# A SwiGLU's gate and up projections by two-by-two blocks with seven products, on the second half of the tokens

## The chip, the cores and the metric

The kernel runs on one core of a Trainium2 chip. The metric is the device time of one execution in microseconds (us), smaller is better. The engines are called by their names: TensorE (PE in the rows) multiplies matrices, VectorE (DVE) and GpSimd (POOL) work elementwise, ScalarE (ACT) computes functions and copies, SyncE (SP) issues transfers (DMAs) between HBM and SBUF. PSUM is the memory that TensorE writes its sums to, in 8 banks.

## What is computed

One step of a hybrid decoder layer for 1024 prompt tokens and 8 sample tokens with a model width of 1024: attention and a recurrent part, an output projection, then a normed, modulated input `h2` to a SwiGLU feed-forward part with 2816 columns:

```python
h2  = modulate(rms_norm(x), ...)
ffn = (silu(h2 @ w_ffn_gate) * (h2 @ w_ffn_up)) @ w_ffn_down   # 1024 -> 2816 -> 1024
x   = x + gate2 * ffn
```

Everything is fp32. The change touches the feed-forward part alone, and of it the second half of the tokens.

## The kernel before, in words

The feed-forward part is computed for two halves of the tokens, one after the other: half A with 512 tokens, half B with 512 prompt tokens and the 8 sample tokens, 520 columns, taken as 256 and 264. The 2816 columns are 22 blocks of 128, worked on in pairs, so 11 pairs for B.

An fp32 product is emulated with three products of a faster format. Every operand is split into a high part (a rounded copy) and a low part (what the rounding left), and high x high, high x low and low x high are added up in PSUM (`mm_fm`, L264 to L272, matmul L270). So each weight tile needs three steps in `wtile`: a load of 512 KB (L1644), ScalarE's high copy (L1648) and the subtraction for the low part (L1649), which `self.loe` does, GpSimd in half B. The same is done to tokens (`h2hi`, `h2lo`) and activations (`ah`, `al`).

For each of a pair's two blocks `ffn` multiplies gate and up weights by the tokens (8 blocks of 128 rows x 3 products x 2 parts of the columns), applies Silu on ScalarE (L1673), multiplies on VectorE out of PSUM (L1674) and splits the result (L1675, L1676). Then come the down products of the pair (L1685, 96 matmuls) and VectorE's additions to eight accumulators (L1696). The last pair of B scales its sums by `gate2` and writes the rows out (`ffn_rows`: transposes L1740, additions L1741, stores L1742).

A's last steps, scaling (L1718) and `ffn_rows`, stand in the code between B's first pair and the others. B's tokens come from `out_part` (L1530 to L1635), which ends with the splitting of the sample tokens at L1635. The code gives each engine's work in an order that a scheduler then rearranges; at run time each engine follows its own order, and semaphores hold it back where a buffer or an input isn't ready. Tiles live in pools; a name has as many buffers as `bufs` says, and a new tile of that name waits until the oldest is no longer read. A pool that is opened after others were closed takes their memory and waits for what used it.

## Time and profile before

| what | us |
|---|---|
| median of 3 runs (lowest to highest) | 2057.04 (2055.04 to 2057.09) |
| the profiled execution | 2053.88 |
| its span in the profile | 2051.8 |
| TensorE busy | 1924.1 (94%) |
| VectorE, ScalarE, GpSimd busy | 1213.6, 808.2, 728.8 |
| gate, up and other products of `mm_fm` on the chain (L270) | 37% |
| down products on the chain (L1685) | 11% |

The profile shows one execution. The span runs from the first to the last recorded instruction; some us of the execution lie outside it. The mean granted clock of TensorE was 0.965 of full speed. Half B's pairs fill the program from about 1650 us to the end, so the stretches of the trace that matter here lie behind 1560 us.

### The profile page before, as it was taken

What the parts mean: (1) busy time and instruction counts of PE and PEld (TensorE: products, weight loads), DVE (VectorE), ACT (ScalarE), POOL (GpSimd) and SP (SyncE); (2) the same over time, 40 slices, a digit from 0 to 9 for tenths busy, and PEclk for the clock granted to TensorE, in tenths of its full rate; (3) what the DMA queues carried; (4) which work ended last, traced back from release to release, by engine and by line L of the source; (5) the groups of instructions that cost most, each with busy time, mean ns of one, the idle gap of its engine ahead of it and who ended that gap; (6) DMA issues with size and microseconds to landing.
All of it is one profiled execution on the core that took longest, in us unless ns stands there. A gap on an engine that the chain in (4) does not pass through costs nothing.

```text
span 2051.8 us, 39068 instructions
## 1 busy us (share of the span) xinstructions
PE 1924.1 (94%) x15050; PEld 1649.1 (80%) x15050; DVE 1213.6 (59%) x3024; ACT 808.2 (39%) x1646; POOL 728.8 (36%) x1347
## 2 busy tenths in 40 slices
PE   4999999999999989899969999999999999999998
PEld 3878898999976667677659777777768989999998
DVE  7777988886646656676645554677644452222225
ACT  5466676643324445455433422322213322222221
POOL 2411244100033456466444303012214444545452
PEclk9999999999998979899979999999999999999999
...
GB/s 265 88 32 31 54 104 104 114 146 91 71 126 188 186 106 49 82 71 45 51 151 93 95 82 131 120 115 141 134 102 222 133 49 154 93 90 93 88 93 112
DMA packets 303720, 220.30 MB, mean 107 GB/s; under 512 B 67663, under 2 KB 282162, under 8 KB 303534
## 3 DMA queue, kind: packets, MB, share of 16 engines
...
q8 instruction: 118, 1.93, 0.4%
...
q10 hardware_dynamic: 18, 0.04, 0.0%
...
## 4 chain that ended last, share of the span: by engine, by line
PE 76%; DVE 10%; DMA 5%; ACT 3%; issue 3%; POOL 1%; SPq 1%; DVEq 0%; ACTq 0%; POOLq 0%
PE ps L270 37%; PE ps L1685 11%; PE ps L1574 5%; PE ps L1272 3%; PE ps L1261 2%; DVE sc L563 2%; PE ps L1062 2%; PE ps L1241 1%; PE ps L973 1%; PE ps L388 1%; PE ps L183 1%; DMA d_x<-ox 1%; DMA d_t<-arr 1%; PE ps L1242 1%; DVE fl L1649 1%
## 5 line engine op out<-in xcount | busy, mean ns | idle before, releaser
L1648 ACT ACTIVATE fh<-fr 128x1024 fp32r<-128x1024 f32 (+1 forms) x183 | 191.6, 1056 | 519.8 <-PE ps L270 289.0
L270 PE MATMUL ps<-h2hi,fh 128*128 128x264 f32 (+2 forms) x1056 | 341.9, 326 | 9.7 <-ACT fh L1648 6.4
L270 PE MATMUL ps<-h2hi,fl 128*128 128x264 f32 (+2 forms) x1056 | 338.0, 325 | 8.7 <-DVE fl L1649 8.7
L270 PE MATMUL ps<-h2lo,fh 128*128 128x512 f32 (+2 forms) x1056 | 340.0, 323 | 0.5 <-POOL h2lo L1623 0.5
L1649 POOL TENSOR_TENSOR fl<-fr,fh 128x1024 fp32r<-128x1024 f32 (+1 forms) x95 | 229.9, 2426 | 283.7 <-ACT fh L1648 277.6
L270 PE MATMUL ps<-h1hi,fh 128*128 128x344 f32 (+1 forms) x752 | 247.9, 330 | 4.0 <-ACT y L932 2.7
L270 PE MATMUL ps<-h1hi,fl 128*128 128x344 f32 (+1 forms) x752 | 244.3, 325 | 0.0
L270 PE MATMUL ps<-h1lo,fh 128*128 128x344 f32 (+1 forms) x752 | 244.3, 325 | 0.0
L270 PEld LDWEIGHTS ps<-h2hi,fh 128*128 128x128 f32 x1056 | 201.8, 191 | 30.9 <-ACT fh L1648 12.8
L270 PEld LDWEIGHTS ps<-h2hi,fl 128*128 128x128 f32 x1056 | 200.5, 191 | 29.5 <-DVE fl L1649 12.1
L270 PEld LDWEIGHTS ps<-h2lo,fh 128*128 128x128 f32 x1056 | 201.7, 191 | 14.5 <-POOL h2lo L1623 0.7
L1025 POOL TENSOR_TENSOR itmp<-la,arr 128x24 f32<-128x24 f32 (+23 forms) x496 | 129.4, 261 | 226.9 <-DMA la<-d_l 191.1
L1674 DVE TENSOR_TENSOR fa<-fa,ps 128x256 f32<-128x256 f32 (+1 forms) x66 | 33.8, 512 | 245.9 <-PE ps L270 245.2
L1685 PE MATMUL ps<-al,fh 128*128 128x512 f32 (+2 forms) x528 | 166.3, 321 | 1.1 <-DVE al L1676 1.0
L1685 PE MATMUL ps<-ah,fl 128*128 128x512 f32 (+2 forms) x528 | 160.7, 320 | 0.0
L1685 PE MATMUL ps<-ah,fh 128*128 128x512 f32 (+2 forms) x528 | 157.1, 322 | 1.2 <-ACT ah L1675 1.2
L1696 DVE TENSOR_TENSOR acc<-acc,ps 128x512 f32<-128x512 f32 (+2 forms) x224 | 107.8, 516 | 82.1 <-PE ps L1685 81.7
L270 PEld LDWEIGHTS ps<-h1hi,fh 128*128 128x128 f32 x752 | 141.4, 188 | 11.0 <-issue 3.6
L1649 DVE TENSOR_TENSOR fl<-fr,fh 128x1024 fp32r<-128x1024 f32 x88 | 108.5, 1233 | 70.1 <-ACT fh L1648 63.9
L1027 POOL TENSOR_TENSOR arr<-arr,itmp 128x24 f32<-128x24 f32 (+23 forms) x496 | 136.0, 274 | 38.3
L270 PEld LDWEIGHTS ps<-h1lo,fh 128*128 128x128 f32 x752 | 141.4, 188 | 4.3 <-issue 4.1
L270 PEld LDWEIGHTS ps<-h1hi,fl 128*128 128x128 f32 x752 | 141.4, 188 | 1.3 <-issue 1.2
...
## 6 DMA issues: line engine op xcount, KB each, us to landing
...
```

Of the source, the lines that this page charges most:

```text
L270: mm = nc.tensor.matmul(ps[:m, :n], a[:, k, wc:wc + m], b[:, k, t0:t0 + n], start=(k == 0 and i == 0), stop=(k == kd - 1 and i == 2))
L563: nc.vector.scalar_tensor_tensor(sc, r[:, :L], wcol, sc, op0=OP.mult, op1=OP.add)
L1025: ie.tensor_tensor(t3, bc(la[:, s, s + 1:][:, None, :], [128, nu, nt]), bc(arr[:, 0:nu, s:s + 1], [128, nu, nt]), op=OP.mult)
L1027: ie.tensor_tensor(arr[:, 0:nu, s + 1:], arr[:, 0:nu, s + 1:], t3, op=OP.subtract)
L1062: nc.tensor.matmul(pd[c % 2][E2[b], 128 * (c // 2):128 * (c // 2) + 128], w[i, c, :], x[i, c, :], start=True, stop=True)
L1261: nc.tensor.transpose(ps[:, 128 * (l % 4):128 * (l % 4) + 128], P[e][:, 128 * l:128 * l + 128], ident)
L1272: nc.tensor.matmul(po[o, 0:128], vt[:, l, o], PT[e][:, 128 * (l % 4):128 * (l % 4) + 128], start=(l == 0), stop=(l == i))
L1574: nc.tensor.matmul(p3[:, t, :], a[:, k, ts], b[:, k % 4, :], start=(k == 0 and n == 0), stop=(k == KD - 1 and n == 2))
L1648: nc.scalar.activation(hi, raw, AF.Copy)
L1649: self.loe.tensor_tensor(lo, raw, hi.bitcast(F32), op=OP.subtract)
L1685: self.lastmm = nc.tensor.matmul(ps[:, :n], a[:, 0, 128 * o:128 * o + 128], b[:, c:c + n], start=(i == 0), stop=(i == 5))
L1696: self.lastv = nc.vector.tensor_tensor(a, a, ps[:, :n], op=OP.add)
```

## The change

In half B the products of gate and up are taken in blocks of two by two: the 1024 rows are cut in two (4 blocks of 128 rows each), the pair's 256 columns in two, and the 520 tokens in two (256 and 264). Strassen's scheme, in the form with 15 additions, needs 7 products of such blocks where the direct way needs 8, and sums of blocks before and after.

- `quad_tokens` makes the sums of the token blocks once (16 additions on VectorE, with high copies on ScalarE and low parts on GpSimd), ahead of the pairs.
- `quad_weights` loads a pair's gate or up weights as one tile of 1 MB, makes four sums of blocks (`fs0` to `fs3`, one buffer each) on VectorE, and yields seven blocks of 128x512 with high and low parts (`fh`, `fl`, 8 buffers each).
- `quad_mm` runs the seven products, 12 matmuls each, and puts the four results together with seven additions on VectorE and one copy on ScalarE; `quad_gate_up` applies Silu, multiplies and splits, now from SBUF and 520 columns at a time.
- The down weights get names of their own (`dr`, `dh`, `dl`, two buffers each). The down products stay.
- B's weight pool `wfB` is opened only after the token sums, A's last rows and the closing of A's pools; all of B's pairs, the first too, stand behind A's rows.

```diff
--- before.py
+++ after.py
@@ -1635,21 +1635,119 @@
             nc.vector.tensor_tensor(lo[:, :, ts], f, hi[:, :, ts].bitcast(F32), op=OP.subtract)
-    def wtile(self, src, r0, c0, nr, ncol, wp):
+    def wtile(self, src, r0, c0, nr, ncol, wp, nm="f", nb=None):
...
-        nb = self.wbufs
-        raw = wp.tile([128, nr, ncol], F32, name="fr", bufs=nb[0])
+        nb = nb or self.wbufs
+        raw = wp.tile([128, nr, ncol], F32, name=nm + "r", bufs=nb[0])
...
-        hi = wp.tile([128, nr, ncol], F32R, name="fh", bufs=nb[1])
-        lo = wp.tile([128, nr, ncol], F32R, name="fl", bufs=nb[2])
+        hi = wp.tile([128, nr, ncol], F32R, name=nm + "h", bufs=nb[1])
+        lo = wp.tile([128, nr, ncol], F32R, name=nm + "l", bufs=nb[2])
         nc.scalar.activation(hi, raw, AF.Copy)
         self.loe.tensor_tensor(lo, raw, hi.bitcast(F32), op=OP.subtract)
         return hi, lo
-    def ffn(self, h, cols, fs, acc, wp, tp, pst, t0=None):
+    N2 = QT + NS
+    def quad_tokens(self, h, pool, tp):
+        nc, n = self.nc, self.N2
+        new = [[pool.tile([128, 4, n], F32R, name=f"q{i}{z}") for z in "hl"] for i in (2, 3, 4)]
+        t1 = [a[:, 0:4, QT:] for a in h]
+        for k in (0, 2):
+            ks = slice(k, k + 2)
+            b = []
+            for i in range(2):
+                for j in range(2):
+                    t = tp.tile([128, 2, n], F32, name=f"qb{i}{j}")
+                    w, kk, c = (n if j else QT), slice(4 * i + k, 4 * i + k + 2), (slice(QT, None) if j else slice(0, QT))
+                    if not j:
+                        nc.vector.memset(t[:, :, QT:], 0.0)
+                    nc.vector.tensor_tensor(t[:, :, 0:w], h[0][:, kk, c].bitcast(F32), h[1][:, kk, c].bitcast(F32), op=OP.add)
+                    b.append(t)
+            t = [tp.tile([128, 2, n], F32, name=f"qt{i}") for i in range(4)]
+            nc.vector.tensor_tensor(t[2], b[3], b[1], op=OP.subtract)
+            nc.vector.tensor_tensor(t[0], b[1], b[0], op=OP.subtract)
+            nc.vector.tensor_tensor(t[1], b[3], t[0], op=OP.subtract)
+            nc.vector.tensor_tensor(t[3], t[1], b[2], op=OP.subtract)
+            for x, (hi, lo) in zip(t, [t1] + new):
+                nc.scalar.activation(hi[:, ks, :], x, AF.Copy)
+                nc.gpsimd.tensor_tensor(lo[:, ks, :], x, hi[:, ks, :].bitcast(F32), op=OP.subtract)
+        return [t1] + new
+    def quad_weights(self, src, f0, wp):
+        nc = self.nc
+        cols = src.shape[-1]
+        raw = wp.tile([128, KD, 2, 128], F32, name="fr", bufs=2)
+        nc.sync.dma_start(raw.rearrange("p k f c -> p k (f c)"),
+                          bass.AP(tensor=src.tensor, offset=src.offset + 128 * f0, ap=[[cols, 128], [128 * cols, KD], [1, 256]]))
+        blk = lambda f, i: raw[:, 4 * i:4 * i + 4, f, :]
+        S = [wp.tile([128, 4, 128], F32, name=f"fs{i}", bufs=1) for i in range(4)]
+        nc.vector.tensor_tensor(S[0], blk(1, 0), blk(1, 1), op=OP.add)
+        nc.vector.tensor_tensor(S[1], S[0], blk(0, 0), op=OP.subtract)
+        nc.vector.tensor_tensor(S[2], blk(0, 0), blk(1, 0), op=OP.subtract)
+        nc.vector.tensor_tensor(S[3], blk(0, 1), S[1], op=OP.subtract)
+        for x in (blk(0, 0), S[1], blk(0, 1), S[2], S[0], S[3], blk(1, 1)):
+            hi = wp.tile([128, 4, 128], F32R, name="fh", bufs=8)
+            lo = wp.tile([128, 4, 128], F32R, name="fl", bufs=8)
+            nc.scalar.activation(hi, x, AF.Copy)
+            self.loe.tensor_tensor(lo, x, hi.bitcast(F32), op=OP.subtract)
+            yield hi, lo
+    def quad_mm(self, src, f0, out, h, T, wp, tp, pst):
+        nc, n = self.nc, self.N2
+        b = lambda i, j: [a[:, 4 * i:4 * i + 4, QT * j:QT * j + (n if j else QT)] for a in h]
+        w = self.quad_weights(src, f0, wp)
+        def prod(x, m):
+            (wh, wl), ps = next(w), pst.tile([128, 512], F32, name="ps")
+            for k in range(4):
+                for i, (u, v) in enumerate(((wh, x[0]), (wh, x[1]), (wl, x[0]))):
+                    nc.tensor.matmul(ps[:, :m], u[:, k, :], v[:, k, 0:m], start=(k == 0 and i == 0), stop=(k == 3 and i == 2))
+            return ps[:, :m]
+        v = nc.vector.tensor_tensor
+        new = lambda nm: tp.tile([128, n], F32, name=nm, bufs=2)
+        self.qn = self.qn + 1
+        m1 = self.qm[self.qn % 2]
+        nc.scalar.activation(m1[:, 0:QT], prod(b(0, 0), QT), AF.Copy)
+        u2, u3, u4 = new("u2"), new("u3"), new("u4")
+        v(u2, m1, prod(T[1], n), op=OP.add)
+        v(out[:, 0, 0:QT], m1[:, 0:QT], prod(b(1, 0), QT), op=OP.add)
+        v(u3, u2, prod(T[2], n), op=OP.add)
+        p5 = prod(T[0], n)
+        v(u4, u2, p5, op=OP.add)
+        v(out[:, 1, QT:], u3, p5, op=OP.add)
+        v(out[:, 0, QT:], u4, prod(b(1, 1), n), op=OP.add)
+        v(out[:, 1, 0:QT], u3[:, 0:QT], prod(T[3], QT), op=OP.subtract)
+    def quad_gate_up(self, f0, h, T, wp, tp, pst):
+        nc, I = self.nc, self.I
+        m = QT + self.N2
+        g = tp.tile([128, 2, m], F32, name="qg", bufs=2)
+        self.quad_mm(I["w_ffn_gate"][0], f0, g, h, T, wp, tp, pst)
+        for f in range(2):
+            nc.scalar.activation(g[:, f, :], g[:, f, :], AF.Silu)
+        u = tp.tile([128, 2, m], F32, name="qu", bufs=2)
+        self.quad_mm(I["w_ffn_up"][0], f0, u, h, T, wp, tp, pst)
+        act = []
+        for f in range(2):
+            ah = tp.tile([128, m], F32R, name="ah", bufs=self.abufs)
+            al = tp.tile([128, m], F32R, name="al", bufs=self.abufs)
+            nc.vector.tensor_tensor(u[:, f, :], u[:, f, :], g[:, f, :], op=OP.mult)
+            nc.scalar.activation(ah, u[:, f, :], AF.Copy)
+            nc.vector.tensor_tensor(al, u[:, f, :], ah.bitcast(F32), op=OP.subtract)
+            act.append((ah, al))
+        return act
+    def ffn(self, h, cols, fs, acc, wp, tp, pst, t0=None, T=None):
...
             act, down = [], []
-            for f in (f0, f0 + 1):
+            if T:
+                act = self.quad_gate_up(f0, h, T, wp, tp, pst)
+            for f in (f0, f0 + 1) if T is None else ():
...
             for f in (f0, f0 + 1):
-                down.append(self.wtile(wd, 128 * f, 0, 1, D, wp))
+                down.append(self.wtile(wd, 128 * f, 0, 1, D, wp, *(("d", (2, 2, 2)) if T else ())))
...
-            fp2 = lpool("wfB")
-            with tc.tile_pool(name="oB", bufs=1) as tp:
+            with tc.tile_pool(name="woB", bufs=1) as fp2, tc.tile_pool(name="oB", bufs=1) as tp:
                 self.out_part([2, 3], hB[0], hB[1], tp, fp2, pb)
             self.loe, self.wbufs, self.abufs = nc.vector, WA, 2
             ffA(FS, NF)
-            self.loe, self.wbufs, self.abufs = nc.gpsimd, WB, 3
-            ap_, tp = lpool("accB"), lpool("tFB")
-            accB = [ap_.tile([128, 2 * QT + NS], F32, name=f"acc{o}") for o in range(KD)]
-            pb = Ring(*([self.psr, self.psa] * 3), self.psc, self.pss)
-            cB = [(0, 256), (256, 264)]
-            self.ffn(hB, cB, range(0, 2, 2), accB, fp2, tp, pb)
+            tq = lpool("tqB")
+            with tc.tile_pool(name="tqS", bufs=1) as tp:
+                tops = self.quad_tokens(hB, tq, tp)
             self.ffn_gate(accA, 512, 512)
             for t in range(4):
                 self.ffn_rows(accA, [t], self.ffn_x([t], fp, WA[0]), 0, pa)
-            self.ffn(hB, cB, range(2, NF, 2), accB, fp2, tp, pb, 4)
             cf.close()
+            fp2 = lpool("wfB")
+            self.loe, self.wbufs, self.abufs = nc.gpsimd, (2, 3, 3), 3
+            ap_, tp = lpool("accB"), lpool("tFB")
+            accB = [ap_.tile([128, 2 * QT + NS], F32, name=f"acc{o}") for o in range(KD)]
+            self.qn, self.qm = 0, [tp.tile([128, self.N2], F32, name=f"qm{i}") for i in range(2)]
+            for m in self.qm:
+                nc.vector.memset(m[:, QT:], 0.0)
+            pb = Ring(*([self.psr, self.psa] * 3), self.psc, self.pss)
+            cB = [(0, 256), (256, 264)]
+            self.ffn(hB, cB, range(0, NF, 2), accB, fp2, tp, pb, 4, tops)
 # ---- launch: one core; inputs and outputs as the reference has them ----
```

SyncE, where the first half's rows are read and stored and the second half's weights are first loaded. `fr_18754` to `fr_19002` are weights of B's first pair, `d_x2` is where `out_part` leaves the residual that A's rows read back. Before:

```order
L1644 DMA fr_18754<-in_w_ffn_gate_dram 128x8x128
L1644 DMA fr_18760<-in_w_ffn_up_dram 128x8x128
L1644 DMA fr_18878<-in_w_ffn_gate_dram 128x8x128
L1644 DMA fr_18884<-in_w_ffn_up_dram 128x8x128
L1644 DMA fr_19002<-in_w_ffn_down_dram 128x1024
L1598 DMA d_x2_80<-oxs_17817 8x1024
L1594 DMA d_x2_80<-ox_17799 128x4x1024
```

After (`fr_18814` and the three like it are A's rows):

```order
L1598 DMA d_x2_80<-oxs_17817 8x1024
L1827 DMA fr_18814<-d_x2_80 128x1024
L1827 DMA fr_18829<-d_x2_80 128x1024
L1842 DMA out_0_dram<-fr_18814 128x1024
L1842 DMA out_0_dram<-fr_18829 128x1024
L1827 DMA fr_18844<-d_x2_80 128x1024
L1827 DMA fr_18859<-d_x2_80 128x1024
L1842 DMA out_0_dram<-fr_18844 128x1024
L1842 DMA out_0_dram<-fr_18859 128x1024
L1688 DMA fr_18900<-in_w_ffn_gate_dram 128x8x256
```

B's weight loads stood ahead of the residual's stores; now the first of them stands behind all of A's row reads and stores.

VectorE, at the end of a pair's gate and up products in the middle of B, before. `fa` is Silu(gate) times up, `ps` a PSUM bank:

```order
L1674 TENSOR_TENSOR fa_19662<-fa_19662,ps_19637 128x256
L1674 TENSOR_TENSOR fa_19717<-fa_19717,ps_19692 128x264
L1674 TENSOR_TENSOR fa_19786<-fa_19786,ps_19761 128x256
L1674 TENSOR_TENSOR fa_19841<-fa_19841,ps_19816 128x264
L1696 TENSOR_TENSOR acc0_18746<-acc0_18746,ps_19858 128x256
L1696 TENSOR_TENSOR acc1_18747<-acc1_18747,ps_19874 128x256
```

After. `qu` and `qg` are up and gate results, `u3` and `u4` parts of them, `fs0` to `fs3` the sums of a weight block for a later product, `al` the low parts of the activation:

```order
L1728 TENSOR_TENSOR qu_19476<-u4_19507,ps_19585 128x264
L1694 TENSOR_TENSOR fs2_19915<-fr_19911 128x512
L1744 TENSOR_TENSOR qu_19476<-qu_19476,qg_19333 128x520
L1729 TENSOR_TENSOR qu_19476<-u3_19506,ps_19603 128x256
L1692 TENSOR_TENSOR fs0_19913<-fr_19911 128x512
L1744 TENSOR_TENSOR qu_19476<-qu_19476,qg_19333 128x520
L1746 TENSOR_TENSOR al_19618<-qu_19476,ah_19617 128x520
L1693 TENSOR_TENSOR fs1_19914<-fs0_19913,fr_19911 128x512
L1746 TENSOR_TENSOR al_19623<-qu_19476,ah_19622 128x520
L1695 TENSOR_TENSOR fs3_19916<-fr_19911,fs1_19914 128x512
L1796 TENSOR_TENSOR acc0_18887<-acc0_18887,ps_19639 128x256
```

Between the last results and the first addition to an accumulator there now stand four sums of weights, two products and two low parts, where there was nothing.

GpSimd in the same pairs, before (`fl` low parts of weights, `al` of activations):

```order
L1649 TENSOR_TENSOR fl_19725<-fr_19722,fh_19724 128x1024
L1649 TENSOR_TENSOR fl_19731<-fr_19728,fh_19730 128x1024
L1676 TENSOR_TENSOR al_19611<-fa_19662,ah_19610 128x256
L1649 TENSOR_TENSOR fl_19849<-fr_19846,fh_19848 128x1024
L1676 TENSOR_TENSOR al_19611<-fa_19717,ah_19610 128x264
L1676 TENSOR_TENSOR al_19735<-fa_19786,ah_19734 128x256
L1649 TENSOR_TENSOR fl_19855<-fr_19852,fh_19854 128x1024
```

After (`dl` low parts of the down weights; the rows after these run on to seven gate blocks and the next up block, then the next `dl`):

```order
L1649 TENSOR_TENSOR dl_20064<-dr_20061,dh_20063 128x1024
L1649 TENSOR_TENSOR dl_20070<-dr_20067,dh_20069 128x1024
L1700 TENSOR_TENSOR fl_19943<-fs1_19914,fh_19942 128x512
L1700 TENSOR_TENSOR fl_19961<-fr_19911,fh_19960 128x512
L1700 TENSOR_TENSOR fl_19979<-fs2_19915,fh_19978 128x512
L1700 TENSOR_TENSOR fl_19997<-fs0_19913,fh_19996 128x512
L1700 TENSOR_TENSOR fl_20016<-fs3_19916,fh_20015 128x512
L1700 TENSOR_TENSOR fl_20034<-fr_19911,fh_20033 128x512
L1700 TENSOR_TENSOR fl_20213<-fr_20202,fh_20212 128x512
L1700 TENSOR_TENSOR fl_20234<-fs1_20205,fh_20233 128x512
L1700 TENSOR_TENSOR fl_20252<-fr_20202,fh_20251 128x512
```

The activations' low parts have left GpSimd, its weight subtractions are halved in size, and there are 16 of them a pair instead of 6.

## Rows read from the trace of the kernel before

**Rows 1.** The page, part 4: chain that ended last, by engine.

```profile
PE 76%; DVE 10%; DMA 5%; ACT 3%; issue 3%; POOL 1%; SPq 1%; DVEq 0%; ACTq 0%; POOLq 0%
```

**Rows 2.** Windows: stretch and length, busy (count) per engine, clock, DMA share, GB/s.

```profile
1735.04:1769.47 34.43, 34.43 (x290) 34.43 (x289) 7.86 (x20) 9.03 (x14) 17.22 (x11) 1.00 0.30 93
1710.00:2030.00 320.00, 320.00 (x2676) 320.00 (x2676) 79.74 (x199) 84.91 (x133) 162.19 (x95) 1.00 0.30 92
```

**Rows 3.** TensorE's timeline: where the last pair's down products begin.

```profile
2029.48 0.28 PE L1685 MATMUL ps<-ah,fh 128*128 128x256 f32 x1
```

**Rows 4.** Lines by form, 1400 to 2052: busy, mean ns, idle before.

```profile
L1649 POOL TENSOR_TENSOR fl<-fr,fh 128x1024 fp32r<-128x1024 f32 x74 | 177.9, 2411 | 160.0 <-ACT fh L1648 153.9 <-issue 6.1
L1623 POOL TENSOR_TENSOR h2lo<-oy,h2hi 128x512 fp32r<-128x512 f32 x8 | 10.6, 1342 | 16.3 <-ACT h2hi L1622 16.3
L1676 DVE TENSOR_TENSOR al<-fa,ah 128x512 fp32r<-128x512 f32 x10 | 6.8, 680 | 0.0
L1696 DVE TENSOR_TENSOR acc<-acc,ps 128x264 f32<-128x264 f32 x72 | 28.5, 426 | 16.5 <-PE ps L1685 16.5
L1741 DVE TENSOR_TENSOR fr<-ps,fr 128x512 f32<-128x512 f32 x16 | 10.6, 689 | 9.5 <-DMA fr<-d_x 7.8 <-PE ps L1740 1.4
L1592 DVE TENSOR_TENSOR oxs<-oxs,oys 8x256 f32<-8x256 f32 x4 | 10.0, 2506 | 0.1
L1648 ACT ACTIVATE fh<-fr 128x1024 fp32r<-128x1024 f32 x102 | 106.6, 1058 | 315.0 <-PE ps L270 162.3 <-PE ps L1685 131.3 <-issue 7.4
L1622 ACT ACTIVATE h2hi<-oy 128x512 fp32r<-128x512 f32 x8 | 5.1, 632 | 13.9 <-DVE oy L1620 13.9
```

**Rows 5.** GpSimd's timeline: start, length, line, operation, count [idle before].

```profile
1561.77 4.75 POOL L1649 TENSOR_TENSOR fl<-fr,fh 128x1024 fp32r<-128x1024 f32 x2
1582.90 4.95 POOL L1649 TENSOR_TENSOR fl<-fr,fh 128x1024 fp32r<-128x1024 f32 x2
1654.71 2.73 POOL L1623 TENSOR_TENSOR h2lo<-oy,h2hi 128x512 fp32r<-128x512 f32 x2 [1.93 <-ACT h2hi L1622]
```

**Rows 6.** VectorE's timeline beside it.

```profile
1584.08 0.41 DVE L1590 TENSOR_TENSOR oys<-ps,oys 8x256 f32<-8x256 f32 x1 [2.50 <-ACT oys L1589]
1584.53 1.07 DVE L1591 TENSOR_TENSOR oys<-oys,ogs 8x256 f32<-8x256 f32 x1
1585.62 2.51 DVE L1592 TENSOR_TENSOR oxs<-oxs,oys 8x256 f32<-8x256 f32 x1
1588.06 0.67 DVE L1674 TENSOR_TENSOR fa<-fa,ps 128x512 f32<-128x512 f32 x1
1651.17 0.48 DVE L1718 TENSOR_SCALAR acc<-acc,modT 128x512 f32<-128x512 f32 x1
1654.80 2.93 DVE L1718 TENSOR_SCALAR acc<-acc,modT 128x512 f32<-128x512 f32 x2
1661.04 0.91 DVE L1635 TENSOR_TENSOR h2lo<-f2s,h2hi 128x64 fp32r<-128x64 f32 x1 [0.32 <-ACT h2hi L1634]
```

**Rows 7.** TensorE's waits from 1560 on: total us, times, longest.

```profile
PE ps L270 <- ACT h2hi L1634: 3.0, 1, 3.0
PE ps L1685 <- ACT ah L1675: 1.2, 1, 1.2
```

**Rows 8.** Windows behind that wait (columns as in rows 2).

```profile
1662.00:1667.00 5.00, 5.00 (x25) 5.00 (x24) 0.42 (x1) 0.80 (x2) 0.73 (x1) 0.50 0.00 0
1667.00:1693.00 26.00, 26.00 (x217) 25.99 (x216) 6.96 (x18) 6.36 (x11) 11.64 (x7) 1.00 0.28 82
```

**Rows 9.** SyncE's timeline: one weight load's issue.

```profile
1780.85 0.38 SPq L1644 DMA_DIRECT2D fr<-in_w_ffn_up_dram  x1
```

**Rows 10.** Windows of that load's data (columns as in rows 2).

```profile
1782.00:1783.50 1.50, 1.50 (x15) 1.50 (x14) 0.42 (x1) 0.18 (x1) 0.00 (x0) 1.00 0.86 243
1783.50:1784.00 0.50, 0.50 (x6) 0.50 (x6) 0.00 (x0) 0.24 (x1) 0.18 (x1) 1.00 1.04 303
1784.00:1785.00 1.00, 1.00 (x10) 1.00 (x9) 0.00 (x0) 0.00 (x0) 0.55 (x1) 1.00 0.04 11
```


## The prediction

> **What bounds the kernel now.** I read the chain of waits first, then the second half of the program (from 1560 us) in windows, then the engines beside TensorE. The chain is TensorE's for 76% of the span [rows 1]. In the windows from 1710 to 2030 us TensorE is busy for all 320.00 us at full clock [rows 2]. One pair of column blocks takes 34.43 us [rows 2], which is 288 matmuls (192 for gate and up, 96 for down), so 34.43 / 288 = 0.1195 us each. Beside it VectorE works 7.86 us, ScalarE 9.03 and GpSimd 17.22 [rows 2]: here each matmul removed is worth its 0.12 us, as long as the others keep up. The last pair's down products start at 2029.48 [rows 3], so 22.3 us before the span's end of 2051.8.
>
> **The change, part by part.**
>
> *Removed.* Of 8 block products for gate and 8 for up, 7 and 7 remain, each of 12 matmuls: 24 fewer per pair, 264 for 288, so 264 x 0.1195 = 31.5 us per pair on TensorE and 2.9 less than now. Over 11 pairs that is 264 matmuls or 31.5 us. This is all that can be won.
>
> *Added work, by its price.* A weight block is now 128x512. Its high part is a ScalarE copy at 0.63 us (the L1622 form) beside 1.06 for the old 128x1024 [rows 4]; 14 of them and two for down make about 11 us of a pair and bind nothing. Its low part is a GpSimd subtraction: half of the old 2.411 us is 1.21, the L1623 row of the same size says 1.34 [rows 4]; I take 1.25, as the old shape with less of a start in it, and keep both ends. A pair has 14 of these (17.5 us) and two low parts of the down weights at 4.75 for both [rows 5]: 22.3 us, where it was 17.22. VectorE gets eight sums of weight blocks, two products with the gate and two low parts of the activations per pair, all of some 512 columns with both inputs in SBUF: 0.68 us for one [rows 4], about 0.61 from start to start as at 1588.06; its other additions read PSUM and take 0.43 [rows 4].
>
> *What these two cost each other.* Where both engines have work, the rows show them shutting each other out. The L1590 addition, which reads PSUM, runs in 0.41 us inside a GpSimd subtraction; the next two, L1591 and L1592, read SBUF twice on only 8x256 elements and take 1.07 and 2.51 us [rows 6]: each ends where one of the two GpSimd instructions of 1582.90 ends [rows 5]. L1592 takes 2.506 us on the mean of four [rows 4], so this is the rule. The L1718 scaling takes 0.48 us alone and 2.93 for two beside the two GpSimd subtractions of 1654.71 [rows 5, 6]. From both I read an alternation: VectorE waits for the GpSimd instruction that runs, then GpSimd, already waiting, goes before VectorE's next. The two GpSimd instructions take 4.95 us with a small VectorE one between them and 4.75 without [rows 5], so changing over costs at most the short instruction itself. The Trainium skill (SBUF — State Buffer, section SBUF: two separate sides) says that the pair of ports is locked for a whole instruction and the other engine fully blocks; the rows agree, but it does not say who is next when both wait. The same page (A bandwidth-pool intuition that's wrong) reports about 0.115 us from VectorE's end until the blocked side goes on, in another setting; nine changes a pair at that price would put the sum about 10 us higher, and the 4.95 us row leaves no room for it.
>
> *A steady pair.* By the program's order the loop through GpSimd is this. The low parts of the down weights have two buffers, so both wait until the pair before has ended its down matmuls, and they stand ahead of this pair's second to seventh up blocks, which stand ahead of the next pair's seven gate blocks and first up block. VectorE has, in its own order, four sums for the next gate, one for the next up (which waits for the fourth gate block's low part), the first product with the gate, another sum (which waits for the fifth), the second product, then the low part of the first activation. TensorE needs that low part after its first 8 down matmuls. From the end of the last downs: 0.9 for the down weight's high part, 4.75, 14 x 1.25 = 17.5, and 9 VectorE instructions x 0.61 = 5.5, together 28.6 us. TensorE has by then done 14 products (168 x 0.1195 = 20.1) and the 8, and has waited 7 to 8 us, in two pieces: before the first down product for the high part (ready about 3.8 us late) and after the 8 matmuls. Then 88 matmuls follow, 10.5 us: 39.1, I use **39.2 us** where it was 34.43. The stall is the new wait that outweighs the removed matmuls, and it stands in front of everything queued on TensorE.
>
> *The clock.* One wait of 3.0 us [rows 7] is followed by 5.0 us at a granted clock of 0.50 with 25 matmuls where some 42 fit, then 1.00 [rows 8]: about 2 us lost. A pair now has two such waits, but the loss counts only in the part after the second one, and a wait of 1.2 us [rows 7] stands in a stretch at full clock. I take 1.5 us a pair, bounds 0 and 3.
>
> *The bridge.* Now TensorE enters the second half's pairs as soon as their tokens are there, at 1661.95 (end of the L1635 row, [rows 6]), with weights loaded long before; the last rows of the first half lie inside it, hidden by matmuls. In the changed program the token sums, those rows and their stores all stand ahead of the first gate load, which takes memory that the sums free: it waits for GpSimd's last low part of them. The sums begin some 3.6 us after 1661.95, behind scalings and row additions on VectorE. They are 16 VectorE instructions with two SBUF inputs (16 x 0.61 = 9.8) and 8 GpSimd ones (8 x 1.34 = 10.7), which alternate, and six row additions at 0.69 [rows 4] that read PSUM and fit mostly beside GpSimd. With 2 to 3 us of waits along the chain that ends at 1689. A 512 KB load issued at 1780.85 [rows 9] still moves in 1783.5 to 1784.0 and is over by then but for a rest of 11 GB/s [rows 10], so 3.2 us; 512 KB more at the 243 GB/s of its body are 2.2, so 5.4 for 1 MB. With the first high part TensorE starts at **1695.5**; bounds 1688 (sums and low parts overlapping) and 1700.
>
> *First and last pair.* The first pair finds GpSimd with nothing done: up to its low activation there are 17 blocks (14, and three of the next pair that alternate in) at 1.25, 4.75 for down, and 15 VectorE instructions at 0.61: 35.2, and 10.5 for the 88 matmuls, so 46 us. The last has no next pair: 20.1 us of products, 2.0 for product, high and low part, then the old ending of 22.3.
>
> *Sum.* 1695.5 + 46 + 9 x 39.2 + 9 x 1.5 + 22.1 + 22.3 = 2152.2 of span; 2053.88 against a span of 2051.8 is 2.1 outside it: 2154.3 for an execution like the profiled one. The median of the runs, 2057.04, lies 3.2 above the profiled one, so I add a little: **2155 us**, about 98 to 100 more than before. By parts: the pairs in the middle cost 9 x (39.2 + 1.5 - 34.43) = 56, the rest is the bridge and the first pair.
>
> **The rivals.**
>
> *VectorE goes first.* If a waiting VectorE instruction gets the port before GpSimd's next, the low activation needs only 11 of the 14 blocks ahead of it: 0.9 + 4.75 + 13.75 + 5.5 = 24.9, plus 10.5 is 35.4 us a pair. Nine pairs save 34, the first about 4, the clock some: **2113**. The rows speak against it, but on few meetings and other shapes.
>
> *No lock that matters.* If strided halves or the finer mix let both engines run, TensorE sets the pace: 20.1, 1.2 until the high part, 96 matmuls 11.5, so 33 us a pair, a first pair of 37 and no slow clock: 2152.2 - 9 x 6.2 - 9 - 13.5 + 2.1 gives 2076, and 2068 with the bridge at 1688. Still slower: a pair that saves 1.4 us in ten places does not pay for a bridge of 30.
>
> *The other side, faster.* This needs one thing more, that the ScalarE and VectorE steps ahead of the down products vanish behind TensorE's next products. With a pair at p and the start at R the end is R + 10p + 42.4 + 2.1; 0.2% under 2053.88 is 2049.8, so R + 10p must be below 2005. At p = 31.5 that asks R below 1690; at R = 1695.5 it asks 31.0, less than the matmuls take. With R at 1688 the time is **2047.5**.
>
> *The clock stays low.* If the two waits of a pair leave all 88 down matmuls at 0.50, that is 10.5 us more instead of 1.5: 2155 + 81, **2236**. In the rows full speed is back after 5 us [rows 8].
>
> *The change does less than it says.* The counts of matmuls are in the program, so the removal is certain; no time equal to before follows from any of the sums unless a saving and the bridge happen to cancel.
>
> **How the numbers follow.** The sum as made: 0.62, between 2130 and 2178 by the ends of its terms (clock -13 to +13, low parts -6 to +13, bridge -7 to +5). VectorE first: 0.15. No lock that matters: 0.10. Low clock: 0.06. Faster: 0.04. Within 0.2%, about what a measurement of this kernel tells from no change: 0.03. To hold 8 in 10 the range takes the first two whole and half of the third: 2080 to 2178. Faster 0.04, same 0.03, slower 0.93.
>
> **What would show it.** In the changed profile, windows of a steady pair should be near 39 to 41 us, with TensorE busy some 32, and its waits should name the low part of the activation (L1746) and the high part (L1745), 3 to 4 us each and nine times. VectorE's L1744, L1692 to L1695 and L1746 should average well over 1 us though they need 0.68, and GpSimd should stand almost without a gap from the down products' end to the low activation. TensorE's first matmul of the second half should stand near 1695, with few before it from 1655 on. The prediction is wrong if those VectorE lines average 0.7 us, if the steady pair is under 36 us, or if the first gate load is issued before 1680.

## The result and the profile after

The changed kernel takes 2161.79 us (median of 4 runs, 2160.52 to 2170.3), the kernel before on the same chip 2057.07: 1.050 times as long, 95% interval 1.046 to 1.055. The profiled execution took 2162.03 with a span of 2160.2. The forecast was 2155, between 2080 and 2178.

Part 1 of the page (busy time, share, instructions), the window of one pair in the middle, and that pair's two ends on ScalarE, which starts the down weight's high copy as soon as the downs of the pair before have freed its buffer:

```profile
PE 1950.0 (90%) x14786; PEld 1661.9 (77%) x14786; DVE 1429.5 (66%) x3288; ACT 860.5 (40%) x1742; POOL 829.4 (38%) x1421
```

```profile
1788.60:1829.28 40.68, 35.74 (x267) 35.23 (x266) 26.74 (x43) 13.42 (x23) 25.32 (x17) 0.87 0.23 78
```

```profile
1785.03 2.01 ACT L1648 ACTIVATE dh<-dr 128x1024 fp32r<-128x1024 f32 x2 [12.76 <-PE ps L1785]
1825.72 1.06 ACT L1648 ACTIVATE dh<-dr 128x1024 fp32r<-128x1024 f32 x1 [12.99 <-PE ps L1785]
```

Where a pair filled TensorE for 34.43 us at full clock [rows 2], it now takes 40.7 with fewer matmuls, at a mean granted clock of 0.87. The nine pairs in the middle run from 1744.57 to 2108.76, 40.47 each.

TensorE's waits from 1640 us on (total, times, longest):

```profile
PE ps L1785 <- ACT ah L1745: 37.6, 11, 3.8
PE ps L1713 <- ACT fh L1699: 23.7, 1, 23.7
PE ps L1785 <- DVE al L1746: 12.6, 11, 2.0
```

The two waits of the forecast, eleven times each, and the bridge. VectorE's lines by form in the same stretch:

```profile
L1694 DVE TENSOR_TENSOR fs<-fr 128x512 f32<-128x512 f32 x22 | 37.5, 1707 | 10.4 <-POOL fl L1700 9.4
L1744 DVE TENSOR_TENSOR qu<-qu,qg 128x520 f32<-128x520 f32 x22 | 35.7, 1623 | 0.1
L1692 DVE TENSOR_TENSOR fs<-fr 128x512 f32<-128x512 f32 x22 | 31.2, 1417 | 6.0 <-DMA fr<-in_w_ffn_gate_dram 6.0
L1746 DVE TENSOR_TENSOR al<-qu,ah 128x520 fp32r<-128x520 f32 x22 | 17.2, 787 | 0.2 <-ACT ah L1745 0.2
```

The same size took 0.68 before [rows 4]. L1746, which the forecast also had well over 1 us, takes 0.79: in the pair below GpSimd has just stopped when it runs. GpSimd and VectorE at the end of that pair's up products, then TensorE:

```profile
1786.17 4.75 POOL L1649 TENSOR_TENSOR dl<-dr,dh 128x1024 fp32r<-128x1024 f32 x2 [15.12 <-ACT dh L1648]
1790.88 1.29 POOL L1700 TENSOR_TENSOR fl<-fs,fh 128x512 fp32r<-128x512 f32 x1
...
1803.95 4.18 POOL L1700 TENSOR_TENSOR fl<-fs,fh 128x512 fp32r<-128x512 f32 x3
1808.10 3.40 POOL L1700 TENSOR_TENSOR fl<-fr,fh 128x512 fp32r<-128x512 f32 x2
```

```profile
1805.27 1.75 DVE L1694 TENSOR_TENSOR fs<-fr 128x512 f32<-128x512 f32 x1 [0.55 <-POOL fl L1700]
1806.94 1.75 DVE L1744 TENSOR_TENSOR qu<-qu,qg 128x520 f32<-128x520 f32 x1
1808.61 0.41 DVE L1729 TENSOR_TENSOR qu<-u,ps 128x256 f32<-128x256 f32 x1
1808.94 1.42 DVE L1692 TENSOR_TENSOR fs<-fr 128x512 f32<-128x512 f32 x1
1810.29 1.77 DVE L1744 TENSOR_TENSOR qu<-qu,qg 128x520 f32<-128x520 f32 x1
1811.98 0.69 DVE L1746 TENSOR_TENSOR al<-qu,ah 128x520 fp32r<-128x520 f32 x1
```

```profile
1809.41 2.10 PE L1785 MATMUL ps<-ah,dh 128*128 128x256 f32 x8 [3.73 <-ACT ah L1745]
1812.72 0.58 PE L1785 MATMUL ps<-al,dh 128*128 128x256 f32 x1 [1.20 <-DVE al L1746]
```

While GpSimd works, VectorE's instructions with two SBUF inputs need 1.4 to 1.8 us and the one that reads PSUM (L1729) 0.41; when GpSimd has no more work (1811.5), the next takes 0.69. GpSimd's 14 blocks stand without a gap from 1790.88 to 1811.50, 20.6 us where 14 x 1.25 are 17.5. L1694 takes 1.71 us on the mean of 22 and L1744 1.62, about 1 us more than alone.

### The profile page after: what moved, and what is told of

It reads as the page before. It is cut to its first block, busy times and chain, and to the rows that moved or that the text cites. A ratio compares the mean times of both kernels' runs of the same rounds, so it can differ in the third digit from the quotient of the medians.

```text
span 2160.2 us, 39186 instructions
## 1 busy us (share of the span) xinstructions
PE 1950.0 (90%) x14786; PEld 1661.9 (77%) x14786; DVE 1429.5 (66%) x3288; ACT 860.5 (40%) x1742; POOL 829.4 (38%) x1421
## 5 line engine op out<-in xcount | busy, mean ns | idle before, releaser
L270 PE MATMUL ps<-h1hi,fh 128*128 128x344 f32 (+1 forms) x752 | 248.5, 331 | 4.0 <-ACT y L932 2.7
L270 PE MATMUL ps<-h1hi,fl 128*128 128x344 f32 (+1 forms) x752 | 244.8, 326 | 0.0
L270 PE MATMUL ps<-h1lo,fh 128*128 128x344 f32 (+1 forms) x752 | 244.8, 326 | 0.0
L1796 DVE TENSOR_TENSOR acc<-acc,ps 128x256 f32<-128x256 f32 (+1 forms) x224 | 107.2, 516 | 79.7 <-PE ps L1785 79.0
L270 PEld LDWEIGHTS ps<-h1hi,fh 128*128 128x128 f32 x752 | 141.9, 189 | 11.0 <-issue 3.6
L270 PE MATMUL ps<-h2hi,fl 128*128 128x512 f32 x352 | 141.5, 406 | 8.7 <-DVE fl L1649 8.7
L270 PE MATMUL ps<-h2hi,fh 128*128 128x512 f32 x352 | 143.3, 407 | 6.3 <-ACT fh L1648 6.3
L270 PEld LDWEIGHTS ps<-h1lo,fh 128*128 128x128 f32 x752 | 142.0, 189 | 4.3 <-issue 4.1
L270 PEld LDWEIGHTS ps<-h1hi,fl 128*128 128x128 f32 x752 | 141.8, 189 | 1.3 <-issue 1.2
L270 PE MATMUL ps<-h2lo,fh 128*128 128x512 f32 x352 | 141.2, 401 | 0.0
L1700 POOL TENSOR_TENSOR fl<-fs,fh 128x512 fp32r<-128x512 f32 x88 | 126.2, 1456 | 1.3 <-ACT fh L1699 1.3
L1649 POOL TENSOR_TENSOR fl<-fr,fh 128x1024 fp32r<-128x1024 f32 (+1 forms) x29 | 71.5, 2468 | 133.3 <-ACT fh L1648 129.2
L1713 PE MATMUL ps<-h2hi,fh 128*128 128x256 f32 (+1 forms) x352 | 100.3, 285 | 23.7 <-ACT fh L1699 23.7
L1785 PE MATMUL ps<-al,dh 128*128 128x256 f32 (+1 forms) x352 | 109.5, 321 | 12.6 <-DVE al L1746 12.6
L1785 PE MATMUL ps<-ah,dl 128*128 128x256 f32 (+1 forms) x352 | 107.2, 315 | 0.0
L1700 POOL TENSOR_TENSOR fl<-fr,fh 128x512 fp32r<-128x512 f32 x66 | 103.7, 1584 | 6.2 <-ACT fh L1699 6.2
```

The source lines that it names most:

```text
L270: mm = nc.tensor.matmul(ps[:m, :n], a[:, k, wc:wc + m], b[:, k, t0:t0 + n], start=(k == 0 and i == 0), stop=(k == kd - 1 and i == 2))
L1649: self.loe.tensor_tensor(lo, raw, hi.bitcast(F32), op=OP.subtract)
L1700: self.loe.tensor_tensor(lo, x, hi.bitcast(F32), op=OP.subtract)
L1713: nc.tensor.matmul(ps[:, :m], u[:, k, :], v[:, k, 0:m], start=(k == 0 and i == 0), stop=(k == 3 and i == 2))
L1785: self.lastmm = nc.tensor.matmul(ps[:, :n], a[:, 0, 128 * o:128 * o + 128], b[:, c:c + n], start=(i == 0), stop=(i == 5))
L1796: self.lastv = nc.vector.tensor_tensor(a, a, ps[:, :n], op=OP.add)
```

## The experiments

Pairs are measured from one down weight's first high copy to the next. Each ratio is to the kernel before on the same chip. The time until the program reaches the change varies by itself: the last L1296 load, ahead of everything that the change touches, is issued at 1511.07 us in the profile before, at 1522.54 in the profile after, and between 1512.64 and 1537.88 in those below. Starts are therefore also given less that shift ("corrected").

**Without the lock, on the sums.** The four sums take a constant in PSUM instead of their second block (the sums are left out; one PSUM bank less for the ring):

```diff
-        nc.vector.tensor_tensor(S[0], blk(1, 0), blk(1, 1), op=OP.add)
-        nc.vector.tensor_tensor(S[1], S[0], blk(0, 0), op=OP.subtract)
+        nc.vector.tensor_tensor(S[0], blk(1, 0), z, op=OP.add)
+        nc.vector.tensor_tensor(S[1], S[0], z, op=OP.subtract)
...
+            self.zp = self.pss.tile([128, 512], F32, name="ps")
```

> Each of the four sums of a weight block now adds a constant that lies in PSUM instead of a second block in SBUF; the sums themselves are left out. Same count, same order, same size of VectorE instructions, but no second SBUF input. Theory (VectorE instructions with two SBUF inputs and GpSimd shut each other out, in alternation): those eight a pair fall from 1.1 to 1.7 us to about 0.68, GpSimd's L1700 from 1.5 to about 1.3 us, a steady pair falls from 40.4 to 35 to 37 us and the time to 2115 to 2130. Rival (it is only that these sums stand in VectorE's order ahead of the activation, and wait for single buffers): the pair stays at 39.5 to 40.5 and the time within 10 us of 2162.

2141.91 us, ratio 1.041 (1.034 to 1.048); the middle pairs take 35.4 to 39.3, 37.2 on the mean. VectorE by form, then two of its products and GpSimd beside the second:

```profile
L1745 DVE TENSOR_TENSOR qu<-qu,qg 128x520 f32<-128x520 f32 x22 | 41.7, 1897 | 0.4
L1693 DVE TENSOR_TENSOR fs<-fr,ps 128x512 f32<-128x512 f32 x22 | 15.0, 682 | 10.8 <-DMA fr<-in_w_ffn_gate_dram 6.1 <-POOL fl L1701 4.6
```

```profile
1830.39 1.77 DVE L1745 TENSOR_TENSOR qu<-qu,qg 128x520 f32<-128x520 f32 x1
1865.75 4.24 DVE L1745 TENSOR_TENSOR qu<-qu,qg 128x520 f32<-128x520 f32 x1
```

```profile
1863.20 3.79 POOL L1701 TENSOR_TENSOR fl<-fs,fh 128x512 fp32r<-128x512 f32 x3
1866.95 2.49 POOL L1701 TENSOR_TENSOR fl<-fr,fh 128x512 fp32r<-128x512 f32 x2
```

With one input in PSUM all 88 sums run in 0.68 beside a busy GpSimd: in these pairs the slow instructions are those that read SBUF twice. That is worth 3.3 us a pair, a little less than the theory asked (35 to 37 us a pair, 2115 to 2130) and far from the rival's 39.5. The product that still reads SBUF twice is now held longer, in some pairs by the running GpSimd instruction and both that follow (4.24 us): the alternation that the prediction read from the rows is not a rule.

**One engine for both.** All low parts of B's weights on VectorE, GpSimd idle:

```diff
-            self.loe, self.wbufs, self.abufs = nc.gpsimd, (2, 3, 3), 3
+            self.loe, self.wbufs, self.abufs = nc.vector, (2, 3, 3), 3
```

> All low parts of the second half's weights on VectorE, GpSimd idle in the steady pairs; VectorE gets 14 x 0.61 + 2 x 1.2 = 11 us more per pair, some 29 us in all. Theory (the lock between the two engines makes the stall): no instruction of VectorE's is held any more, a pair falls to 34 to 35.5 us and the time to 2100 to 2115. Rival (too much elementwise work, whoever does it): VectorE becomes the bound, the pair stays at 39 us or more and the time at 2155 or above.

2122.05 us, ratio 1.030 (1.024 to 1.036), pairs of 36.9 on the mean (35.9 to 38.8): faster than with two engines, but not the 34 to 35.5 and 2100 to 2115 of the theory.

```profile
L1700 DVE TENSOR_TENSOR fl<-fs,fh 128x512 fp32r<-128x512 f32 x88 | 60.4, 687 | 2.2 <-ACT fh L1699 1.6
L1744 DVE TENSOR_TENSOR qu<-qu,qg 128x520 f32<-128x520 f32 x22 | 15.3, 695 | 0.1
```

```profile
PE ps L1785 <- ACT ah L1745: 25.9, 11, 3.6
```

No instruction is held any more, and TensorE still waits 2.4 us a pair for the activation. So the lock is not all of it. What is left points at the order: the next pair's sums and low parts stand ahead of this pair's activation, on whichever engine. That is tested further down.

**The clock.** 44 matmuls that nobody reads, issued ahead of the down products:

```diff
+        ps = pst.tile([128, 512], F32, name="ps")
+        for i in range(44):
+            nc.tensor.matmul(ps[:, 0:264], self.wl_[:, i % 4, :], T[3][0][:, i % 4, 0:264], start=True, stop=True)
```

> 44 matmuls per pair that nobody reads stand between the up products and the down products, where TensorE waited 3.4 us (44 x 0.12 = 5.3 us). Theory (TensorE loses about 3 us a pair because the clock is halved after the wait, and the wait itself is set by VectorE and GpSimd): granted clock near 1.00 in the pairs, the pair falls from 40.4 to 37.5, the time to about 2135. Rival (the slow stretch behind the wait has another cause, or TensorE is the bound after all): the pair stays at 40.4 or grows by up to 5 us, 2160 to 2215.

2143.18 us, ratio 1.041 (1.034 to 1.047), pairs of 38.1 to 38.2: doing more is 2.3 us a pair faster. What it takes away stands in the windows of the changed kernel's pair (columns as in rows 2):

```profile
1810.00:1818.00 8.00, 6.80 (x31) 6.50 (x31) 4.48 (x6) 0.64 (x1) 1.50 (x1) 0.50 0.41 131
1820.00:1826.00 6.00, 6.00 (x52) 6.00 (x51) 4.38 (x12) 0.28 (x1) 0.00 (x0) 1.00 0.01 3
```

Behind the wait of 3.73 us the granted clock is 0.50 (1.2 GHz) until 1818; 31 matmuls fit into those 8 us, which hold the second wait of 1.20, and 52 into six us at full clock. The mean clock over 320 us, in the changed kernel and then with the filler:

```profile
1710.00:2030.00 320.00, 277.87 (x2075) 273.19 (x2074) 215.48 (x337) 106.84 (x177) 207.61 (x130) 0.89 0.25 83
1710.00:2030.00 320.00, 311.62 (x2532) 307.81 (x2533) 230.63 (x350) 110.29 (x183) 221.71 (x140) 0.99 0.26 85
```

**The down weights' low parts** on VectorE, to take 4.75 us out of GpSimd's chain:

```diff
-        self.loe.tensor_tensor(lo, raw, hi.bitcast(F32), op=OP.subtract)
+        (nc.vector if nm == "d" else self.loe).tensor_tensor(lo, raw, hi.bitcast(F32), op=OP.subtract)
```

> Only the two low parts of the down weights move from GpSimd to VectorE. Theory (GpSimd's chain from the last downs to the activation is what counts, the two at its head take 4.75 us): GpSimd begins the up blocks some 2.5 to 4 us earlier, the pair falls to 37 to 38.5 us and the time to 2130 to 2145. Rival (VectorE's own order is the bound): 2.4 us more on VectorE, pair 40 to 42, time 2160 to 2180.

2167.52 us, ratio 1.052 (1.046 to 1.058), pairs of 39.7 to 41.0: nothing gained, and the rival's numbers. GpSimd's timeline in a pair that began at 1909.20, when the downs ahead of it freed their weights, then ScalarE's step ahead of the high part that GpSimd waits for at 1924.86:

```profile
1911.81 2.00 POOL L1700 TENSOR_TENSOR fl<-fs,fh 128x512 fp32r<-128x512 f32 x1 [17.64 <-ACT fh L1699]
...
1924.86 1.30 POOL L1700 TENSOR_TENSOR fl<-fs,fh 128x512 fp32r<-128x512 f32 x1 [2.15 <-ACT fh L1699]
...
1931.54 3.37 POOL L1700 TENSOR_TENSOR fl<-fr,fh 128x512 fp32r<-128x512 f32 x2
```

```profile
1923.62 0.64 ACT L1737 ACTIVATE qg<-qg 128x520 f32<-128x520 f32 x1 [2.27 <-DVE qg L1729]
```

It starts its blocks 3.2 us earlier after the downs (2.6 for 5.8) and then waits for high parts. The wait of 2.15 us leads back to VectorE: on ScalarE that high part stands behind the Silu (L1737), which waits 2.27 us for VectorE's last gate result, and that stands behind VectorE's sums. GpSimd ends 25.7 us after 1909.20; in the changed kernel that was 26.5. This theory fell: without the 4.75 us the path runs through VectorE's order and is about as long.

**The order alone.** First the sums of the next pair's up weights are held behind this pair's last low activation (L1746) on VectorE; then, in another kernel, the sums for the next gate and GpSimd's low parts of both as well. `issue_after` puts an instruction behind another one in the order of its engine. The helper:

```diff
+    def behind(self):
+        return self.tc.issue_after(self.lasta.ins) if self.lasta is not None else ExitStack()
...
+        with self.behind():
+            nc.vector.tensor_tensor(S[0], blk(1, 0), blk(1, 1), op=OP.add)
...
+            with self.behind():
+                self.loe.tensor_tensor(lo, x, hi.bitcast(F32), op=OP.subtract)
```

> Only an order on VectorE is changed: the four sums for the next pair's up weights now stand behind this pair's activation instead of ahead of it; everything else is as in the changed kernel. Theory as revised after the run that moved the down weights' low parts (the activation is late because those sums, held by GpSimd and waiting for single buffers, stand ahead of it): the wait for the high part of the activation falls from 3.4 to 0.5 to 2 us, the pair from 40.5 to 35 to 37.5 us, the time to 2110 to 2130. Rival (the lock finds the activation itself just as well, GpSimd working beside it): pair 39 us or more, 2150 or above.

> The sums and the low parts of the next pair's gate weights, too, stand behind this pair's activation, so that GpSimd has nothing to do while VectorE makes the activation, and works during the down products, where it stood idle for 15 us a pair. Theory: no instruction of the activation is held, TensorE goes through, clock 1.00, the pair comes to 32 to 33.5 us (31.5 of matmuls) and the time to 2075 to 2095. Rival (16 low parts a pair are too much for GpSimd in what is left, TensorE then waits for gate weights): the pair stays above 36 us.

2116.24 us, ratio 1.026 (1.021 to 1.032), pairs of 35.5 to 36.1; and 2092.41, ratio 1.016 (1.010 to 1.022), pairs of 32.8 to 32.9, both as expected. The second one's waits, a window of 320 us in its pairs, and a GpSimd gap:

```profile
PE ps L1720 <- ACT fh L1700: 23.6, 1, 23.6
PE ps L1792 <- ACT ah L1752: 6.0, 11, 1.0
```

```profile
1710.00:2030.00 320.00, 311.07 (x2547) 306.94 (x2546) 206.91 (x409) 127.97 (x216) 235.66 (x157) 1.00 0.30 99
```

```profile
1849.70 2.54 POOL L1702 TENSOR_TENSOR fl<-fr,fh 128x512 fp32r<-128x512 f32 x2
1860.94 1.29 POOL L1702 TENSOR_TENSOR fl<-fs,fh 128x512 fp32r<-128x512 f32 x1 [8.71 <-ACT fh L1700]
```

GpSimd now pauses while VectorE makes the activation; TensorE's waits for it are 1.0 us at most, and the granted clock is 1.00. A pair is 1.57 us shorter than before the change. The sums are still held where they do meet GpSimd (L1694 1.09 us on the mean), but in the middle pairs TensorE does not wait for that. The edit changes only orders, but with them it also takes away the meetings of the two engines ahead of the activation (its products average 0.71 us where they took 1.62). What the order is worth without the lock was not run. What is left is the bridge, a wait of 23.6 us, and a longer ending.

**The last rows.** In the changed kernel the ending from the last pair's downs (2129.88) takes 30.3 us, before 22.3 [rows 3]. Its row loads share two buffers (`fr`, two of 1 MB) where there were three (of 512 KB): the third and fourth row are loaded only behind the stores of the first two. SyncE and VectorE in the changed kernel:

```profile
2141.16 0.93 SPq L1842 DMA_DIRECT2D out_dram<-fr  x2
2145.73 1.55 SPq L1827 DMA_DIRECT2D fr<-d_x  x2
```

```profile
2149.50 1.29 DVE L1841 TENSOR_TENSOR fr<-ps,fr 128x512 f32<-128x512 f32 x2 [4.25 <-DMA fr<-d_x]
2155.86 1.28 DVE L1841 TENSOR_TENSOR fr<-ps,fr 8x512 f32<-8x512 f32 x2 [3.31 <-DMA fr<-d_x]
```

Two of each four rows were given the idle `dr` buffers:

```diff
-            x = op_.tile([128, D], F32, name="fr", bufs=nb)
+            x = op_.tile([128, D], F32, name=("fr", "fr", "dr", "dr")[t % 4] if t > 3 else "fr", bufs=nb)
```

> The last pair's five row loads go to four buffers instead of the two that the weights leave them. Theory (the ending took 30.3 us from the first of the last down products to the end, where it had been 22.3, because three rows wait for two buffers): ending 22 to 25 us, time 5 to 8 us lower than the changed kernel. Rival (the rows wait for something else, the stores or the additions): ending 29 to 31 us, no change.

2155.41 us, ratio 1.045 (1.038 to 1.051), not separable from the change by the ratios. In the trace the stretch from the end of the last-but-one pair's downs to the end falls from 51.4 us (2108.76 to 2160.2) to 46.1 (2114.75 to 2160.9), and the ending from 30.3 to 25.0 (from 2135.87), the upper end of what was expected.

**The bridge alone.** All that the change puts ahead of the pairs, then the old pairs of 288 matmuls (the gate and up of half B read some sums in place of tokens):

```diff
-            self.ffn(hB, cB, range(0, NF, 2), accB, fp2, tp, pb, 4, tops)
+            self.ffn(hB, cB, range(0, NF, 2), accB, fp2, tp, pb, 4)
```

> The bridge alone: the pairs of half B run as before the change, 288 matmuls each with the weight buffers of before, while everything that the change puts ahead of them stays (the token blocks, their five sums and low parts, and a pool for them); the tokens that they read are in part the sums, so the output's half B is not the reference's. My theory: what the change does ahead of the pairs costs on its own. Corrected for the later start of the unchanged part, the first product of half B started at 1686.9 in the changed kernel, against 1661.3 before, so about 25 us, of which nothing is given back by pairs of 34.4 us: near 2085 (2075 to 2098 with the drift of the unchanged part). Pairs of 34.4, and L1700's waits as before. Rival: the pairs behind the bridge hide it (weights are ready, the engines that feed have time in hand), then the time is within 10 us of before, 2057 to 2067.

2093.73 us where the kernel before took 2067.85, ratio 1.012 (1.007 to 1.016), some 24 us (15 to 33); by the traces, corrected for the shift, the span is 29.2 longer (2094.8 - 13.8 - 2051.8). Windows of its pairs and its first product:

```profile
1750.00:2030.00 280.00, 280.00 (x2344) 280.00 (x2343) 63.42 (x161) 74.01 (x115) 140.45 (x83) 1.00 0.31 93
```

```profile
1700.24 0.58 PE L270 MATMUL ps<-h2hi,fh 128*128 128x256 f32 x1 [23.61 <-ACT fh L1648]
```

Nothing behind it hides it: TensorE is full in the pairs and stays as late as it started. Eleven pairs at 1.57 give back 17 us, so with this bridge the change loses even with the best order.

**A shorter bridge.** Four versions on top of the order above, with the rows' buffers, raw weight buffers opened ahead of the token sums, and the tokens' low parts on VectorE. In three, the first pair stays plain (288 matmuls) and covers part of the token sums. e8 loads that pair's weights late; e10 loads them early and moves the last gate scaling behind the gate product; e11 is e10 without a plain pair; e12 is e10 with half A's rows ahead of the plain pair. The core of it:

```diff
+                self.ffn(hB, cB, range(0, 2, 2), accB, fp2, tp, pb)
...
-                nc.gpsimd.tensor_tensor(lo[:, ks, :], x, hi[:, ks, :].bitcast(F32), op=OP.subtract)
+                nc.vector.tensor_tensor(lo[:, ks, :], x, hi[:, ks, :].bitcast(F32), op=OP.subtract)
...
-            self.ffn(hB, cB, range(0, NF, 2), accB, fp2, tp, pb, 4, tops)
+            self.ffn(hB, cB, range(2, NF, 2), accB, fp2, tp, pb, 4, tops)
```

> The order of the run before last (gate behind the activation), the four row buffers, and a shorter bridge: the second half's first pair is computed in the plain way with 288 matmuls, the token sums stand beside its down products, their low parts on VectorE, and the first blocked weights load into memory that waits for neither. Theory (the bridge is the token sums and the load behind them, both can be hidden): TensorE stands 5 to 10 us instead of some 25, ten blocked pairs take 32 to 33.5 us each, time 2030 to 2050, 0.2 to 1.3% under the kernel before. Rival (the sums and the half clock behind them cost as much as ever): 2060 to 2075.

> The seven products with all of what the runs so far found: the pair's low activation ahead of the next pair's sums on VectorE and of its low parts on GpSimd, the last rows in four buffers, the first pair plain (288 matmuls) with its weights loaded in good time (a pool on the other side of SBUF, ahead of the out projection), the raw weight buffers opened ahead of the token sums, the token low parts on VectorE, and the scaling of the last pair's gate behind the gate product. Theory: in e8 the plain pair waited 14.5 us for its weights at its first product and 11.3 us ahead of it; with the weights there, most of the 26 us go, less what the sums of the tokens, now with the plain pair's low parts beside them, take: 2045 to 2066, best about 2055, so no clear gain and no clear loss; pairs of 32.9, ten of them. Rival: the token sums on VectorE now stand ahead of the plain pair's conversions and products, and TensorE waits as long as before: 2070 to 2085.

> The same without a plain pair: eleven pairs of seven products in the order of e6, the last rows in four buffers, raw weight buffers opened ahead of the token sums, token low parts on VectorE, the last scaling behind the gate product. e6 gave 2092 with 32.86 us a pair; rows save about 5 and the earlier raw loads and token low parts about 10 to 15 of the bridge: 2068 to 2080. Rival: the bridge is not set by the raw loads and the low parts but by the sums of the tokens and of the first weights on VectorE one after the other: 2085 or more.

> As e10, and half A's gate scaling and rows (32 transposes, their adds, loads and stores) are written ahead of the plain pair instead of behind it. In e10 TensorE waited 11.3 us at the first of the seven products, for a high part that waited for the padding of two tiles, which waited 2.85 us for a store of half A's rows: the tiles lie where the rows were. Theory: with the rows stored some 15 us earlier, the first product starts soon after the plain pair's downs, 8 to 11 us sooner, and the time is 0.4 to 0.5% below e10: ratio 0.995 to 0.998 to the kernel before, the first version with the seven products that is faster. Rival: the rows' transposes and adds now stand among the plain pair's products and VectorE's sums of the tokens and cost there what they save (0.999 to 1.003).

| run | median us | ratio to before (95%) |
|---|---|---|
| e8 | 2083.01 | 1.012 (1.007 to 1.017) |
| e10 | 2074.97 | 1.000 (0.997 to 1.003) |
| e11 | 2073.91 | 1.003 (1.000 to 1.005) |
| e12 | 2070.67 | 1.003 (1.000 to 1.006) |

Their middle pairs all take 32.8 to 32.9. e8 missed its expectation, and its rival's too: TensorE waited 11.3 us for the plain pair's weights and 14.5 at the first of the seven products. e10 missed its 2045 to 2066 and lies in its rival's range, though the kernel before took 2067.85 beside it, some 10 us more than beside the changed kernel; e11 came out as expected. e10, e11 and e12 come out at no change; none is shown to be faster. In e10 the first of the seven products waits 11.3 us, behind this on VectorE:

```profile
1729.42 0.07 DVE L2041 MEMSET qm<- 128x8 f32 x1 [2.85 <-DMA out_dram<-fr]
```

Taking that away (e12) moved the wait: its rival held. TensorE in e12:

```profile
1710.93 0.39 PE L1720 MATMUL ps<-h2hi,fh 128*128 128x256 f32 x1 [2.38 <-ACT fh L1700]
...
1723.38 0.59 PE L1720 MATMUL ps<-q2l,fh 128*128 128x264 f32 x1 [3.78 <-DVE q2l L1680]
```

Corrected for the shift the first product starts at 1701.4 for 1703.4 in e10, and the products behind it now wait for the tokens' low parts.

## Why the prediction was right, point by point

| term | forecast, us | trace, us |
|---|---|---|
| TensorE's start of half B's pairs | 1695.5 | 1698.26, corrected 1686.8 |
| first pair | 46 | 46.3 (to 1744.57) |
| nine pairs with the clock | 366.3 | 364.2 (to 2108.76) |
| last products | 22.1 | 21.1 (to 2129.88) |
| ending | 22.3 | 30.3 |
| span | 2152.2 | 2160.2, corrected 2148.7 |

*Which engines shut each other out.* Right. The lock was shown by taking one SBUF input away (e1, 0.68 us for 1.1 to 1.7) and by taking GpSimd away (e2, 0.69). The Trainium skill (SBUF — State Buffer, section SBUF: two separate sides) says that it concerns, among others, VectorE instructions with two SBUF inputs against GpSimd instructions that read SBUF; e1's rows agree. The step from two meetings to a strict alternation was too wide (4.24 us in e1), though in the pair shown of the changed kernel it held, and VectorE first (2113) did not occur.

*A steady pair.* Right in sum: 27.6 us from the down weight's high copy (1785.03) to the low activation's end (1812.67), for 28.6; then 13.0 for the 88 matmuls, for 10.5 and 1.5 of clock. Three sizes were off. VectorE's turns cost GpSimd 20.6 - 17.5 = 3.1 us for eight of them, 0.4 each, not 9 x 0.61. The clock costs 2.3 by the filler, near my upper bound of 3. And of TensorE's waits the one for the low part is 1.1 us on the mean, not 3 to 4. What the sum did not say is that its terms are not separable: taking the 4.75 us away changed nothing (e4), while a new order, which the sum took as given, is worth 7.6 us a pair (e6, which also ends the meetings ahead of the activation). The first pair's 46.3 for 46 is luck in part: its low activation is there 34 us after the start, for 35.2, and the rest takes 12.3 for 10.5: the sum gave this pair no slow clock, and the granted clock was 0.83 from 1726 to 1746 us.

*The bridge.* Right in kind, 8.7 us early, corrected. First sum, last low part, the first gate load and the first product in the changed kernel:

```profile
1669.41 0.67 DVE L1671 TENSOR_TENSOR qb<-h2hi,h2lo 128x512 f32<-128x512 f32 x1
1690.81 1.29 POOL L1680 TENSOR_TENSOR q4l<-qt,q4h 128x528 fp32r<-128x528 f32 x1 [1.32 <-ACT q4h L1679]
1692.13 0.39 SPq L1688 DMA_DIRECT2D fr<-in_w_ffn_gate_dram  x1
1698.26 0.58 PE L1713 MATMUL ps<-h2hi,fh 128*128 128x256 f32 x1 [23.70 <-ACT fh L1699]
```

The sums and their low parts took 22.7 us (1669.41 to 1692.10) for my 23.4, and the load to its first use (1692.13 to 1697.57) the 5.4 of the forecast. The step that failed is the start: I took 1661.95 for the last tokens from the kernel before; they are there at 1657.0, corrected, and the sums begin 0.9 us later, not 3.6. Most of the 4.9 us arises in the out projection: its last L1577 starts at the same time in both, corrected, and its last L1592 ends 3.8 us earlier. Before, GpSimd made low parts of half B's first weights there and L1592 took 2.51 us [rows 4]; in the changed kernel the last one stands beside an idle GpSimd:

```profile
1638.44 0.41 DVE L1592 TENSOR_TENSOR oxs<-oxs,oys 8x256 f32<-8x256 f32 x1
```

A second reading was wrong: the prediction (and e9's expectation) has TensorE enter half B's pairs only when the last tokens are there. In the kernel before, it had 48 of the first pair's 288 matmuls done by then (L270 alone; matmuls, weight loads, clock, DMA):

```profile
1649.00:1660.90 11.90, 6.69 (x48) 5.95 (x48) 0.98 0.01 1
```

So the bridge costs more than the 25 us between the two starts. Measured by itself (e9) it is 29 us by the trace and 24 by the runs, which allow 15 to 33.

*The ending.* The step "the old ending of 22.3" failed, by 8.0: the change takes the weight buffers `fr` from three to two, and the prediction does not ask who else takes tiles of that name. The last rows do. e7 gives 5.3 of it back.

*The sum.* The early start (-8.7) and the long ending (+8.0) cancel, so the corrected span is 3.5 under the forecast; 11.5 us later start of unchanged work put the measured time above it. That the total came so close is luck in part. Of the cost over before by the trace, 2148.7 - 2051.8 = 97, the nine pairs are 54 (9 x 6.04), the ending is 8, and the start, the first pair and the last products together are the other 35.

*The rivals.* The lock matters, the clock is back at full some 8 us after the wait, and faster was not reached, even with the order, the ending and the bridge repaired. The reasoning against the last one, that a pair saving 1.4 us does not pay for a bridge of 30, is what e6 (1.57) and e9 (24 to 29) measured.
